# A hybrid decoder layer on one core: two buffers for K and Q, a freed second output tile, an early load for the last tile, S1 x T1 ahead, and statistics that are spread by transposes

## The chip, the cores and the metric

The kernel runs on one core of one Trainium2 chip. The core has a matrix engine (TensorE, PE in the profile, with its weight loads as PEld), a vector engine (VectorE, DVE), a scalar engine (ScalarE, ACT), GpSimd (POOL) and SyncE (SP), which here issues nearly all DMA transfers. Each engine takes its own instructions in order and waits for the others by semaphores. The metric is the time of one execution in microseconds (us) of device time, as the median of several runs. Beside the runs there is one profiled execution, which has its own time.

## The reference

One decoder layer, 2048 tokens by 1024 channels, float32. What is computed, cut to what matters here:

```
u    = rmsnorm(x) ;  proj = u @ w_in          # hq, hf, hi, hg (4 heads x 128 each), att q/k/v
f    = lb + (1 - lb) * sigmoid(hf)            # per head h: q, k = 1 - f, v, log f
S_t  = diag(f_t) S_{t-1} + k_t v_t^T ;  o_t = S_t^T q_t        # HGRN2, four heads
o_hg = rmsnorm(o) * silu(hg)
o_att = sliding-window (128) attention, 8 query heads over 2 key heads, a sink logit per head
h    = x + concat(o_hg, o_att) @ w_out
v    = rmsnorm(h)
gate = causal depthwise conv(v @ w_gate)
h    = h + (silu(gate) * (v @ w_up)) @ w_down
out  = rmsnorm(h)
```

## The kernel before

Activations lie transposed, channels on the 128 partitions and tokens along the free dimension. The sequence is done in two halves of 1024 tokens (`HALF`), one after the other, with the same program; the recurrent state, a key/value block and the convolution's halo are carried over. Every float32 operand of a large product is split into a high and a low part in a reduced format (`split`, `split_into`, `prep`: a cast on ACT, a subtraction on DVE), and a product is then three TensorE instructions (high x high, high x low, low x high), each of 128 x 128 weights by 512 columns.

A half has these stages. (1) The input is loaded and split, and its sum of squares collected. (2) Two key/value units, then for each of four heads a HGRN2 head (`hgrn`) and a pair of attention heads (`attend`), as Python generators that are stepped by turns. (3) `out_proj`: eight output tiles d = 0 to 7, each one `unit` of 48 TensorE instructions (tile `pop`) over the eight mixed tiles M in the order 0, 4, 1, 5, 2, 6, 7, 3; M[3] and M[7] come from the last head (h = 3) and the last attention pair (j = 3). (4) `gate_up`: eleven pairs of feed-forward tiles, each pair a gate and an up product; a pair product (`pair_unit`) computes a 2 x 2 block product in seven products of 12 instructions (a Strassen-Winograd form, with operands B11, T1, B21, T2, T3, B22, T4 on the activation side and A11, S1, A12, S2, S3, S4, A22 on the weight side). (5) `down`: the same form for w_down, with the activations reloaded from device memory, and the final norm.

A HGRN2 head makes K = 1 - f and Q = q * f in two tiles, and then walks seven levels (m = 1, 2, 4 ... 64): at each, ACT copies part of K into G (levels below 32), TensorE multiplies G or K by Q (tile `plev`), and DVE multiplies K and Q by decays and copies the masked result into ST. Afterwards K is transposed (`pkn`), the states are chained (`pu`, SS), and `po` takes ST and Q. K and Q had one buffer each, so a head's Q could only be written after the `po` of the head before. In the attention pair, scores (`psc`) are exponentiated, transposed (`ppt`), masked by DVE into `po` and `pp` (line 395) and multiplied by V (`poT`).

In `out_proj` the input tile of output tile d (`h0` to `h7`, from `xT`) takes one of eight slots of a ring, tag `m`. Weight operands of the gate's first pair are made in the middle of tile d = 6 by `prep_pair`, and one of them, S4's two parts, took a slot of that ring before `h7`; `h7` came after it.

What sets the order: the program is written in one order per engine by a scheduler that simulates a timeline, from the dependencies, the buffers and the order of the code. `tc.issue_after` holds a block behind a given instruction. `AFTER` (line 37) did that for two units of `out_proj`: d = 1 behind level 8 of the last head, d = 2 behind its `po`.

The norm's statistics (`Stats`): squares are added into `acc` over the channels' tiles; `inverse` (lines 232 to 244) sums over partitions on TensorE (`pst`, one column per 128 tokens), takes the inverse root on DVE in thirteen small instructions (`rsqrt`), and writes a diagonal matrix per 128 tokens; `spread` (lines 246 to 255) multiplies ones by it (`pinv`), which puts the tokens' factors on all partitions. For the gate, `inverse` was put ahead of product S2 x T2 of the first pair and `spread` ahead of S4 x B22 (the table `then`, line 762).

Of the kernel before, what the change touches and what calls it, by code (L numbers as in the profile page):

```python
# [17 lines left out]
P = 128  # L18
# [15 lines left out]
QUADS = ["A11", "A12", "A21", "A22"]  # L34
PRODUCTS = [("P1", "A11", "B11"), ("P5", "S1", "T1"), ("P6", "S2", "T2"), ("P3", "S4", "B22"),
            ("P7", "S3", "T3"), ("P2", "A12", "B21"), ("P4", "A22", "T4")]
AFTER = {1: 8, 2: "po"}
LEVELS = [1, 2, 4, 8, 16, 32, 64]
NEG = -1.0e30
UT = 7  # L40
# [5 lines left out]
def hymba_layer(ctx: ExitStack, tc: tile.TileContext, a: dict, out: bass.AP):  # L46
# [18 lines left out]
    def ps(kind, name):  # L65
        return spaces[kind].tile([P, 512], F32, tag=kind, name=name)
# [79 lines left out]
        nc.vector.tensor_scalar(C.omlb, C.lb, -1.0, 1.0, op0=ALU.mult, op1=ALU.add)  # L146


    def rsqrt(ss, n, scale, keep=None):

        ms = sp.tile([P, n], F32, tag=f"ms{n}", name="ms")
        nc.vector.tensor_scalar(ms, ss, scale, EPS, op0=ALU.mult, op1=ALU.add)
        y = sp.tile([P, n], F32, tag=f"y{n}{keep}", name="y")
        yi = y.bitcast(I32)
        nc.vector.tensor_scalar(yi, ms.bitcast(I32), 1, None, op0=ALU.logical_shift_right)
        nc.vector.tensor_scalar(yi, yi, -1.0, float(0x5F3759DF), op0=ALU.mult, op1=ALU.add)
        nc.vector.tensor_scalar(ms, ms, -0.5, None, op0=ALU.mult)
        t = sp.tile([P, n], F32, tag=f"t{n}", name="t")
        for _ in range(3):
            nc.vector.tensor_tensor(t, y, y, op=ALU.mult)  # L160
            nc.vector.tensor_tensor(t, t, ms, op=ALU.mult)
            nc.vector.scalar_tensor_tensor(y, t, 1.5, y, op0=ALU.add, op1=ALU.mult)
        return y

    def raw4(src):
# [49 lines left out]
    class Stats:  # L215
# [16 lines left out]
        def inverse(self, keep):  # L232

            n = self.acc.shape[-1]
            nt = n // P
            st = ps("hg", "pst")
            for c in range(nt):
                nc.tensor.matmul(st[:, c:c + 1], self.acc[:, c * P:(c + 1) * P], ones[:, 0:1],
                                 start=True, stop=True)
            rs = self.rs = rsqrt(st[:, 0:nt], nt, 1.0 / D, keep)  # L240
            dg = self.acc
            return nc.vector.tensor_tensor(dg.rearrange("p (c t) -> p c t", t=P),
                                    ident.unsqueeze(1).to_broadcast([P, nt, P]),
                                    rs.unsqueeze(2).to_broadcast([P, nt, P]), op=ALU.mult)

        def spread(self, bank=None):

            n = self.acc.shape[-1]
            w = min(n, 512)
            for b in range(n // w):  # L250
                pb = ps(aux[b % 2 if bank is None else bank], "pinv")[:, 0:w]
                nc.tensor.matmul(pb, ones, self.acc[:, b * w:(b + 1) * w], start=True, stop=True)
                if bank is not None:
                    return pb
                nc.scalar.copy(self.acc[:, b * w:(b + 1) * w], pb)
# [161 lines left out]
    def hgrn(hf, h, X, invb, vs, WG, mix, p, fu=None):  # L417
# [9 lines left out]
            nc.vector.scalar_tensor_tensor(q[:, bs], qu[b], 128.0 ** -0.5, invb[:, bs], op0=ALU.mult, op1=ALU.mult)  # L427
        nc.vector.tensor_scalar(f, f, C.omlb[:, h:h + 1], C.lb[:, h:h + 1], op0=ALU.mult, op1=ALU.add)
        yield
        K = p.tile([P, HALF], F32, tag="K", name="K", bufs=1)  # L430
        nc.vector.tensor_scalar(K, f, -1.0, 1.0, op0=ALU.mult, op1=ALU.add)
        Q = p.tile([P, HALF], F32, tag="Q", name="Q", bufs=1)
        nc.vector.tensor_tensor(Q, q, f, op=ALU.mult)


# [7 lines left out]
                                    ident.unsqueeze(1).to_broadcast([P, 4, P]), op=ALU.mult)  # L443


        late = h == HG - 2

        def gate():
            gu = unit(WG.get(h, a["w_g"][h]), X, "g")
# [73 lines left out]
                                               op0=ALU.mult, op1=ALU.add)  # L523
        yield
        g = q
        if h < HG - 2:
            gate()
            yield
        on = p.tile([P, TT, P], F32, tag="t4", name="on", bufs=2)
# [74 lines left out]
    def out_proj(hf, M, p):  # L604

        order = [0, 4, 1, 5, 2, 6, 7, 3]
        lo, hi = slice(0, 512), slice(512, HALF)
        acc = inv_tile()
        st = Stats(acc)
        sts = [Stats(acc[:, bs], lambda: p.tile([P, 512], F32, tag="ut", name="sq", bufs=UT)) for _, bs in halves()]  # L610
        ops = Operands(p)
        ops.get("B11", 0)
        kept, v = [], []
        W = [prep(a["w_out"][d], d == 2) for d in range(3)]
        first = None
        for d in range(KT):
            t = slot(f"h{d}")
            nc.sync.dma_start(t, a["xT"][d, :, hf * HALF:(hf + 1) * HALF])
            if d == KT - 2:
                W += [prep(a["w_out"][k]) for k in (d, d + 1)]  # L620

                first = prep_pair(a["w_gate"][0], a["w_gate"][1],
                                  lambda n: p.tile([P, D], F32R, tag="ga", name=n, bufs=2),
                                  lambda n: p.tile([P, 512], F32, tag="ut", name=n, bufs=UT))
            if d >= len(W):
                W.append(prep(a["w_out"][d]))
            with tc.issue_after(marks[AFTER[d]].ins) if d in AFTER else ExitStack():
                o = unit(W[d], M, "pop", order, "at" if d == 2 else "mm", in_turn=d == KT - 1)
            k = dp.tile([P, HALF], F32, name=f"keep{hf}{d}")
            kept.append(k)  # L630
            u = v[d - 4] if d >= 4 else None
            w = [t[:, bs] if d < KT - 1 else p.tile([P, 512], F32, tag="ut", name="v7", bufs=UT) for _, bs in halves()]
            for b, bs in halves():
                nc.vector.tensor_tensor(t[:, bs], t[:, bs], o[b], op=ALU.add)
                sts[b].add(t[:, bs])
                nc.sync.dma_start(k[:, bs], t[:, bs])
                nc.scalar.activation(w[b], t[:, bs], AF.Identity, scale=C.nfw[:, d:d + 1])
                if d >= 4 and b == 0:
                    split_into(*ops.get("B21", d - 4), w[0])
            v.append(t)  # L640
            if d < 4:
                split_into(*ops.get("B11", d), t[:, lo])
                t1 = p.tile([P, 512], F32, tag="ut", name="t1", bufs=UT)
                nc.vector.tensor_tensor(t1, t[:, hi], t[:, lo], op=ALU.subtract)
                split_into(*ops.get("T1", d), t1)
                continue

            nc.vector.tensor_tensor(u[:, hi], w[1], u[:, hi], op=ALU.subtract)
            nc.vector.tensor_tensor(u[:, lo], u[:, hi], u[:, lo], op=ALU.add)
            nc.vector.tensor_tensor(w[0], w[0], u[:, lo], op=ALU.subtract)  # L650
        for op, base, part in (("T2", 0, lo), ("T3", 0, hi), ("B22", 4, hi), ("T4", 4, lo)):
            for i in range(4):
                split_into(*ops.get(op, i), w[op == "B22"] if base + i == KT - 1 else v[base + i][:, part])
        return kept, ops, st, first

    def prep_pair(src1, src2, home=None, ut=None):
# [8 lines left out]
        def m(name, shape=[P, D], dt=F32R):  # L665
            return hp.tile(shape, dt, tag="m", name=name, bufs=KT)
# [22 lines left out]
            split_into(*A, r1)  # L689
        R = ring()  # L690
        split_into(*R, r2)
        dd = m("S4", [P, 2, 512])
        split_into(dd[:, 0], dd[:, 1], S4)
        cut = lambda t, c: (t[0][:, c], t[1][:, c])
        return {"A11": cut(A, lo), "A12": cut(A, hi), "S1": cut(B, lo), "S2": cut(B, hi),
                "S3": cut(R, lo), "A22": cut(R, hi), "S4": (dd[:, 0], dd[:, 1])}

    def pair_unit(W, ops, p, evac, then={}):

        def prod(o, w, t, more=False):
            wh, wl = W[w]
            then.pop(w, lambda: None)()
            for i in range(4):
                xh, xl = ops.get(t, i)
                ws = slice(i * P, (i + 1) * P)
                nc.tensor.matmul(o, wh[:, ws], xh, start=i == 0 and not more, stop=False, skip_group_check=more)  # L708
                nc.tensor.matmul(o, wh[:, ws], xl, start=False, stop=False, skip_group_check=more)  # L709
                nc.tensor.matmul(o, wl[:, ws], xh, start=False, stop=i == 3, skip_group_check=more)  # L710

        def out(o, name):
            t = p.tile([P, 512], F32, tag="ut", name=name, bufs=UT)
            nc.scalar.copy(t, o)  # L714
            return t

        X = ps("mm", "X")
        prod(X, "A11", "B11")
        s1 = out(X, "s1")
        Z = ps("at", "Z")  # L720
        prod(Z, "A12", "B21")
        evac(0, 0, Z, s1)
        prod(X, "S2", "T2", True)
        u2 = out(X, "u2")
        Y = ps("hg", "Y")
        prod(Y, "S1", "T1")
        s5 = out(Y, "s5")
        prod(X, "S3", "T3", True)
        u3 = out(X, "u3")
        evac(1, 1, u3, s5)  # L730
        prod(Y, "S4", "B22", True)
        evac(0, 1, Y, u2)
        prod(X, "A22", "T4", True)
        evac(1, 0, X, None)

    def gate_up(hf, ops, hs, nxt, p):
# [5 lines left out]
        for pr in range(FT // 2):  # L742
# [14 lines left out]
            def flush():  # L757
                while later:
                    later.pop(0)()

            later = []
            then = {"S2": lambda: hs.inverse("h"), "S4": lambda: (hs.spread(), flush())} if pr == 0 else {}
            nxt = prep_pair(srcs[2 * pr + 1][0], srcs[2 * pr + 1][1])
            pair_unit(W, ops, p, gate, then)
            flush()
            ys = []
            for i in range(2):
# [323 lines left out]
```

## Time and profile before

| what | value |
|---|---|
| runs | 2214.91, 2217.16, 2218.22 us; median 2217.16 us |
| profiled execution, its own time | 2213.91 us |
| its span in the trace | 2212.2 us |
| TensorE busy | 2175.0 us (98%) |
| VectorE busy | 1638.0 us (74%) |
| ScalarE busy | 1049.3 us (47%) |
| chain that ended last | PE 95%, DVE 3%, ACT 1%, DMA 1% |
| HBM traffic over the span | 252 MB, 114 GB/s |

How to read it: an engine's busy time counts its instructions, and for TensorE their ends are modelled. Rows of the timeline give the start, the length, the engine and line, the operation with its output and inputs (buffer numbers left out), and in brackets the idle time before it with what ended that. Rows by windows give, for each stretch, the busy time and instruction count of PE, PEld, DVE, ACT and POOL, then the granted TensorE clock (PEclk, 1.00 is full), the DMA share and GB/s. By their columns, the gate of the first half begins at 462 us, that of the second at 1555 us; `out_proj` begins at 343 and 1427 us.

### The profile page before, as it was taken

The numbers are of one execution on the slowest core, as the hardware profiler recorded it, in microseconds if no ns is written. First come the engines' busy times: TensorE is split into PE (matmuls) and PEld (weight loads), VectorE is DVE, ScalarE is ACT, GpSimd is POOL, SyncE is SP. The second block draws the span as 40 slices with busy tenths as digits, with TensorE's granted clock in tenths as the row PEclk, the third lists the DMA queues.
The fourth block names the chain that finished last, engine by engine and source line by source line (L and its number), as shares of the span: only waits on it lengthen the run. The fifth ranks groups of instructions, "written<-read, shape, count | busy, mean of one in ns | idle before, by whom it ended". The sixth has DMA issues, their size and how long they took to land.

```text
span 2212.2 us, 29221 instructions
## 1 busy us (share of the span) xinstructions
PE 2175.0 (98%) x11302; PEld 1822.3 (82%) x11302; DVE 1638.0 (74%) x2458; ACT 1049.3 (47%) x1825; POOL 14.4 (1%) x37
## 2 busy tenths in 40 slices
PE   8999998999999999999999999999999999999997
PEld 6988987778888888888889889878788888888887
DVE  6567567688887888775865666667878888887766
ACT  5445454454444445335725455535534444443353
POOL 2000000000000000000000000000000000000000
PEclk9999999999999999999999999999999999999999
DMA  4111112323333234964631111113232323359643
GB/s 154 39 29 39 29 29 77 108 83 93 113 100 115 87 128 145 376 230 159 203 124 38 30 29 39 59 37 136 64 125 86 125 85 119 95 194 393 220 130 128
DMA packets 89995, 254.15 MB, mean 115 GB/s; under 512 B 11008, under 2 KB 13184, under 8 KB 89856
## 3 DMA queue, kind: packets, MB, share of 16 engines
q1 hardware_dynamic: 87552, 251.17, 34.1%
q8 instruction: 88, 1.44, 0.3%
q10 hardware_dynamic: 2304, 1.12, 0.2%
q14 instruction: 51, 0.42, 0.1%
HBM read 195.10 MB, written 57.15 MB: 114 GB/s over the span
## 4 chain that ended last, share of the span: by engine, by line
PE 95%; DVE 3%; ACT 1%; DMA 1%; issue 0%; ACTq 0%; DVEq 0%
PE X L708 7%; PE X L709 7%; PE X L710 7%; PE pop L197 6%; PE q L197 4%; PE hq L197 4%; PE f L197 4%; PE pdx L890 4%; PE pdx L891 4%; PE Y L708 4%; PE pdx L892 4%; PE Y L710 4%; PE Y L709 4%; PE g L197 4%; PE pdy L891 3%; PE pdy L890 3%
## 5 line engine op out<-in xcount | busy, mean ns | idle before, releaser
L585 ACT CAST whi<-raw 128x1024 fp32r<-128x1024 f32 x88 | 92.7, 1053 | 109.7 <-PE X L709 68.8
L709 PE MATMUL X<-T,whi 128*128 128x512 f32 x352 | 137.4, 390 | 0.0
L708 PE MATMUL X<-T,whi 128*128 128x512 f32 x352 | 137.1, 389 | 0.0
L710 PE MATMUL X<-T,wlo 128*128 128x512 f32 x352 | 137.0, 389 | 0.0
L774 DVE SCALAR_TENSOR_TENSOR y<-ga,cw,y 128x1024 f32<-128x1024 f32 x88 | 112.4, 1277 | 28.2 <-ACT y L772 28.1
L714 ACT COPY u<-X 128x512 f32<-128x512 f32 x88 | 51.5, 585 | 122.3 <-PE X L710 122.2
L586 DVE TENSOR_TENSOR wlo<-raw,whi 128x1024 fp32r<-128x1024 f32 x88 | 107.0, 1216 | 0.0
L586 DVE TENSOR_TENSOR xld<-raw,xhd 128x1024 fp32r<-128x1024 f32 x72 | 80.5, 1129 | 18.9 <-ACT xhd L585 18.3
L178 ACT CAST whi<-raw 128x1024 fp32r<-128x1024 f32 (+2 forms) x61 | 62.9, 1035 | 65.9 <-PE hq L197 11.8
L585 ACT CAST xhd<-raw 128x1024 fp32r<-128x1024 f32 x72 | 69.7, 979 | 40.2 <-DMA raw<-act1T 14.4
L197 PE MATMUL pop<-XH,wlo 128*128 128x512 f32 x256 | 83.3, 391 | 0.7 <-DVE wlo L179 0.7
L197 PE MATMUL pop<-XL,whi 128*128 128x512 f32 x256 | 84.0, 392 | 0.0
L197 PE MATMUL pop<-XH,whi 128*128 128x512 f32 x256 | 82.9, 396 | 0.4 <-ACT XH L208 0.2
L179 DVE TENSOR_TENSOR wlo<-raw,whi 128x1024 fp32r<-128x1024 f32 (+2 forms) x61 | 72.9, 1199 | 13.9 <-ACT whi L178 13.9
L708 PEld LDWEIGHTS X<-T,whi 128*128 128x128 f32 x352 | 66.1, 188 | 14.0 <-ACT u L714 0.3
L710 PEld LDWEIGHTS X<-T,wlo 128*128 128x128 f32 x352 | 66.1, 188 | 13.9 <-issue 0.2
L709 PEld LDWEIGHTS X<-T,whi 128*128 128x128 f32 x352 | 66.1, 188 | 13.8 <-issue 0.2
L890 PE MATMUL pdx<-xhd,hid 128*128 128x512 f32 x192 | 74.4, 391 | 1.0 <-ACT hid L585 1.0
L891 PE MATMUL pdx<-xld,hid 128*128 128x512 f32 x192 | 74.8, 390 | 0.0
L708 PE MATMUL X<-T,Sh 128*128 128x512 f32 x176 | 69.0, 392 | 5.2 <-ACT s L714 5.2
L892 PE MATMUL pdx<-xhd,lod 128*128 128x512 f32 x192 | 73.7, 389 | 0.0
L578 PE MATMUL pvv<-whi,XL 128*128 128x256 f32 x256 | 73.2, 287 | 0.0
(363 smaller groups left out, 6544.5 us busy)
## 6 DMA issues: line engine op xcount, KB each, us to landing
wr<-in_w_down SPq DMA_DIRECT2D x90, 512.0 KB, 5.2
raw<-in_w_gate SPq DMA_DIRECT2D x44, 512.0 KB, 3.7
raw<-in_w_up SPq DMA_DIRECT2D x44, 512.0 KB, 3.6
raw<-act0T SPq DMA_DIRECT2D x20, 512.0 KB, 5.6
raw<-act1T SPq DMA_DIRECT2D x20, 512.0 KB, 5.3
act0B<-y SPq DMA_DIRECT2D x33, 256.0 KB, 2.4
act1B<-y SPq DMA_DIRECT2D x33, 256.0 KB, 2.4
raw<-in_w_out SPq DMA_DIRECT2D x16, 512.0 KB, 3.7
```

The costliest lines, as they stand in the source:

```text
L179: nc.vector.tensor_tensor(lo[:, c], raw[:, c], hi[:, c].bitcast(F32), op=ALU.subtract)
L197: nc.tensor.matmul(o[b], w, x[:, bs], start=f, stop=l)
L578: nc.tensor.matmul(o[:, 0:256], xl[:, t], hi[:, c], start=False, stop=False)
L585: nc.scalar.copy(h, src)
L586: (eng or nc.vector).tensor_tensor(l, src, h.bitcast(F32), op=ALU.subtract)
L708: nc.tensor.matmul(o, wh[:, ws], xh, start=i == 0 and not more, stop=False, skip_group_check=more)
L709: nc.tensor.matmul(o, wh[:, ws], xl, start=False, stop=False, skip_group_check=more)
L710: nc.tensor.matmul(o, wl[:, ws], xh, start=False, stop=i == 3, skip_group_check=more)
L774: nc.vector.scalar_tensor_tensor(y, g[:, w:w + HALF], C.cw[:, ft, w:w + 1], y, op0=ALU.mult, op1=ALU.add)
L890: nc.tensor.matmul(o, wh[:, i, c], ah[:, i, cols], start=f, stop=False, skip_group_check=more)
L891: nc.tensor.matmul(o, wh[:, i, c], al[:, i, cols], start=False, stop=False, skip_group_check=more)
L892: nc.tensor.matmul(o, wl[:, i, c], ah[:, i, cols], start=False, stop=l, skip_group_check=more)
```

## The change

Six edits:

- K and Q have two buffers each.
- `AFTER` no longer holds tile d = 1; tile d = 2 stays behind `po`.
- S4's parts for the gate's first pair get a tile of their own (`dd`), so `h7` takes the ring's slot and its load comes ahead of the last two w_out loads.
- In the first gate pair of each half, S1 x T1 is done directly after A11 x B11, ahead of A12 x B21.
- There `inverse` stands ahead of S3 x T3 and `spread` ahead of A22 x T4, one or two products later than before.
- `inverse` writes no diagonal matrix, and `spread` transposes each column of the inverse roots, read with a step of zero 128 times, in place of the product with ones. This is so for all nine spreads of the program.

Another line (`late`) reads differently and has the same value.

```diff
-AFTER = {1: 8, 2: "po"}
+AFTER = {2: 'po'}
...
         def inverse(self, keep):
...
-            rs = self.rs = rsqrt(st[:, 0:nt], nt, 1.0 / D, keep)
-            dg = self.acc
-            return nc.vector.tensor_tensor(dg.rearrange("p (c t) -> p c t", t=P),
-                                    ident.unsqueeze(1).to_broadcast([P, nt, P]),
-                                    rs.unsqueeze(2).to_broadcast([P, nt, P]), op=ALU.mult)
+            self.rs = rsqrt(st[:, 0:nt], nt, 1.0 / D, keep)
+            return made[-1]
...
-                nc.tensor.matmul(pb, ones, self.acc[:, b * w:(b + 1) * w], start=True, stop=True)
+                for c in range(w // P):
+                    i = b * w // P + c
+                    nc.tensor.transpose(pb[:, c * P:(c + 1) * P], self.rs[:, i:i + 1].to_broadcast([P, P]), ident)
...
-        K = p.tile([P, HALF], F32, tag="K", name="K", bufs=1)
+        K = p.tile([P, HALF], F32, tag="K", name="K", bufs=2)
...
-        Q = p.tile([P, HALF], F32, tag="Q", name="Q", bufs=1)
+        Q = p.tile([P, HALF], F32, tag="Q", name="Q", bufs=2)
...
-        late = h == HG - 2
+        late = h in (2,)
...
-        if h < HG - 2:
+        if not late and h < HG - 1:
             gate()
...
-                                  lambda n: p.tile([P, D], F32R, tag="ga", name=n, bufs=2),
+                                  lambda n, shape=[P, D]: p.tile(shape, F32R, tag="dd" if n == "dd" else "ga", name=n,
+                                                                 bufs=1 if n == "dd" else 2),
...
-        dd = m("S4", [P, 2, 512])
+        dd = (home or m)("dd" if home else "S4", [P, 2, 512])
...
         s1 = out(X, "s1")
+        Y = ps("hg", "Y")
+        if ahead:
+            prod(Y, "S1", "T1")
         Z = ps("at", "Z")
         prod(Z, "A12", "B21")
         evac(0, 0, Z, s1)
         prod(X, "S2", "T2", True)
         u2 = out(X, "u2")
-        Y = ps("hg", "Y")
-        prod(Y, "S1", "T1")
+        if not ahead:
+            prod(Y, "S1", "T1")
...
-            then = {"S2": lambda: hs.inverse("h"), "S4": lambda: (hs.spread(), flush())} if pr == 0 else {}
+            then = {"S3": lambda: hs.inverse("h"), "A22": lambda: (hs.spread(), flush())} if pr == 0 else {}
...
-            pair_unit(W, ops, p, gate, then)
+            pair_unit(W, ops, p, gate, then, pr == 0)
```

The change moves instructions on every engine, since the scheduler orders the whole program anew. Three places matter below.

First, TensorE where the last head's levels and the last attention pair meet the first output tiles, first half. `pop` is an output tile, `plev` a level, `ppt` the transposes of the scores, `poT` their product with V. Before, from the second level on:

```order
L469 MATMUL plev_2943<-Q_2916,G_2944 128x2x64 x4
L392 MATMUL ppt_3337<-ident_87,sc_3028 128x128 x4
L392 MATMUL ppt_3346<-ident_87,sc_3028 128x128 x4
L469 MATMUL plev_2955<-Q_2916,G_2956 128x2x64 x4
L197 MATMUL pop0_3501<-XH_3295,whi_3482 128x512
L197 MATMUL pop1_3502<-XH_3295,whi_3482 128x512
L403 MATMUL poT_3353<-po_3335,V_436 64x128
```

In the change 20 `pop` rows stand between the second `ppt` and the third level, and from there on:

```order
L470 MATMUL plev_2960<-Q_2921,G_2961 128x2x64 x4
L199 MATMUL pop0_3506<-XL_3301,whi_3487 128x512
L199 MATMUL pop1_3507<-XL_3301,whi_3487 128x512
L199 MATMUL pop0_3506<-XH_3300,wlo_3488 128x512
L199 MATMUL pop1_3507<-XH_3300,wlo_3488 128x512
L199 MATMUL pop0_3506<-XH_3304,whi_3487 128x512
L199 MATMUL pop1_3507<-XH_3304,whi_3487 128x512
L199 MATMUL pop0_3575<-XL_3301,whi_3493 128x512
L199 MATMUL pop1_3576<-XL_3301,whi_3493 128x512
L199 MATMUL pop0_3575<-XH_3300,wlo_3494 128x512
L404 MATMUL poT_3358<-po_3340,V_441 64x128
```

So between `ppt` and the first `poT` there were one level and two `pop` instructions, and there are now one level and 29. In the second half it is one level and none before, and one level and 33 now. The number of `pop` instructions ahead of the last head's `po` is 84 in both.

Second, ACT at the start of the gate, first half, where `s1` is the copy of the first product, `sq` and `v7` the square and the weighted form of `h7`'s halves. Before:

```order
L585 CAST Sh_4230<-S_4229 128x1024
L227 ACTIVATE sq_4113<-h7_4057 128x512
L637 ACTIVATE v7_4110<-h7_4057,nfw_325 128x512
L227 ACTIVATE sq_4121<-h7_4057 128x512
L637 ACTIVATE v7_4111<-h7_4057,nfw_325 128x512
L714 COPY s1_4258<-X_4245 128x512
L585 CAST B21_4044<-v7_4110 128x512
```

In the change:

```order
L586 CAST T4_4176<-h6_3950 128x512
L229 ACTIVATE sq_4126<-h7_4062 128x512
L639 ACTIVATE v7_4116<-h7_4062,nfw_325 128x512
L716 COPY s1_4263<-X_4250 128x512
L586 CAST Sh_4235<-S_4234 128x1024
```

The first half of `h7` has moved 14 rows up, between casts of T2, and B21's last cast stands before the copy; 1024 columns of `Sh` have moved behind it.

Third, TensorE at the spread of the gate, first half. Before:

```order
L709 MATMUL X_4245<-T4_4172,whi_3980 128x512
L710 MATMUL X_4245<-T4_4171,wlo_3981 128x512
L708 MATMUL X_4245<-T4_4171,whi_3980 128x512
L252 MATMUL pinv_4344<-invb_3478,ones_83 128x512
L252 MATMUL pinv_4347<-invb_3478,ones_83 128x512
L709 MATMUL X_4245<-T4_4172,whi_3980 128x512
```

In the change:

```order
L710 MATMUL Y_4265<-B22_4164,dd_3989 128x512
L711 MATMUL Y_4265<-B22_4165,dd_3989 128x512
L712 MATMUL Y_4265<-B22_4164,dd_3989 128x512
L253 MATMUL pinv_4361<-ident_87,y_4319 128x128 x4
L253 MATMUL pinv_4367<-ident_87,y_4319 128x128 x4
L710 MATMUL Z_4445<-B21_3861,whi_4230 128x512
L711 MATMUL Z_4445<-B21_3862,whi_4230 128x512
```

Two products of 512 columns have become eight transposes of 128. Before, they stood near the end of A22 x T4; now they stand directly behind S4 x B22.

More of the change, by code (lines that the diff above doesn't have):

```diff
@@ L146, in constants @@
         nc.vector.tensor_scalar(C.omlb, C.lb, -1.0, 1.0, op0=ALU.mult, op1=ALU.add)
+    made = []
     def rsqrt(ss, n, scale, keep=None):
@@ L161, in rsqrt @@
             nc.vector.tensor_tensor(t, t, ms, op=ALU.mult)
-            nc.vector.scalar_tensor_tensor(y, t, 1.5, y, op0=ALU.add, op1=ALU.mult)
+            made.append(nc.vector.scalar_tensor_tensor(y, t, 1.5, y, op0=ALU.add, op1=ALU.mult))
         return y
@@ L696, in prep_pair, with pair_unit @@
                 "S3": cut(R, lo), "A22": cut(R, hi), "S4": (dd[:, 0], dd[:, 1])}
-    def pair_unit(W, ops, p, evac, then={}):
+    def pair_unit(W, ops, p, evac, then={}, ahead=False):
         def prod(o, w, t, more=False):
```

## The prediction

> **What bounds the kernel now.** I read the page first (span, busy times, the chain by engine).
>
> ```profile
> span 2212.2 us, 29221 instructions
> PE 2175.0 (98%) x11302; PEld 1822.3 (82%) x11302; DVE 1638.0 (74%) x2458; ACT 1049.3 (47%) x1825; POOL 14.4 (1%) x37
> PE 95%; DVE 3%; ACT 1%; DMA 1%; issue 0%; ACTq 0%; DVEq 0%
> ```
>
> TensorE is the bound: 37.2 us of the span are not PE. A gain can come from three places only: idle time of PE, stretches at a low granted clock, and PE instructions that go. So I went through the span by windows (columns as told above), looking for stretches that are not full:
>
> ```profile
> 351.00:355.00 4.00, 2.73 (x22) 2.23 (x20) 4.00 (x8) 3.74 (x6) 0.00 (x0) 1.00 0.00 0
> 355.00:358.80 3.80, 0.66 (x4) 0.19 (x2) 3.80 (x6) 0.11 (x1) 0.00 (x0) 1.00 0.00 0
> 358.80:362.20 3.40, 3.30 (x28) 2.87 (x27) 3.40 (x6) 0.62 (x1) 0.00 (x0) 0.50 0.00 0
> 377.00:381.00 4.00, 3.04 (x67) 2.52 (x61) 3.96 (x8) 1.30 (x3) 0.00 (x0) 1.00 0.00 0
> 462.24:484.60 22.36, 19.54 (x92) 15.59 (x91) 21.32 (x42) 12.97 (x23) 0.00 (x0) 1.00 0.26 90
> 550.00:600.00 50.00, 50.00 (x222) 41.41 (x221) 42.73 (x57) 21.17 (x30) 0.00 (x0) 1.00 0.37 122
> 1446.00:1451.00 5.00, 2.51 (x17) 1.71 (x16) 5.00 (x8) 2.19 (x3) 0.00 (x0) 1.00 0.00 0
> 1451.00:1454.40 3.40, 3.40 (x28) 2.81 (x30) 3.40 (x5) 0.56 (x1) 0.00 (x0) 0.50 0.16 16
> 1560.00:1562.60 2.60, 0.01 (x1) 0.01 (x1) 2.60 (x5) 2.60 (x6) 0.00 (x0) 1.00 0.53 202
> 1563.70:1567.10 3.40, 3.40 (x13) 2.82 (x11) 3.40 (x7) 0.62 (x1) 0.00 (x0) 0.50 0.31 122
> 1600.00:1650.00 50.00, 50.00 (x222) 41.44 (x221) 42.04 (x56) 20.17 (x29) 0.00 (x0) 1.00 0.38 123
> ```
>
> The gate away from its start is full, 222 products in 50 us or 0.225 us each (0.227 between starts in the rows below). The holes lie where the last head meets the first output tiles (351 and 1446) and where the gate begins (462 and 1560). After three of these four waits the granted clock is 0.50 for 3.4 us, which costs a further 1.7 us each. Those are the two places at which the change moves instructions.
>
> **T1: last head and first output tiles.** The timeline of the first half, and then of the second:
>
> ```profile
> 322.02 1.23 DVE L433 TENSOR_TENSOR Q<-hg,f 128x1024 f32<-128x1024 f32 x1 [3.50 <-PE po L537]
> 351.63 1.09 PE L392 MATMUL ppt<-ident,sc 128*128 128x128 f32 x8 [0.25 <-DVE sc L365]
> 356.47 0.68 DVE L395 TENSOR_TENSOR po<-ppt,ownT 128x512 f32<-128x512 f32 x1
> 358.50 1.41 PE L403 MATMUL poT<-po,V 128*64 128x128 f32 x7 [3.14 <-DVE pp L395]
> 1445.58 1.03 PE L392 MATMUL ppt<-ident,sc 128*128 128x128 f32 x8
> 1450.97 0.98 PE L403 MATMUL poT<-po,V 128*64 128x128 f32 x3 [2.33 <-DVE pp L395]
> ```
>
> From the last transpose (351.63 + 1.09 = 352.72) to the masked scores' first use (358.50) DVE needs 5.8 us, full all the while, and PE has one level and two output products. In the second half it is 1446.61 to 1450.97, 4.4 us, with no product. The freed tile d = 1 puts 29 and 33 products there: 29 x 0.227 = 6.6 us with a level of some 1 us behind or among them is 7.6, and 33 x 0.227 + 1 is 8.5. Both are longer than DVE's time, so the waits of 3.14 and 2.33 us should go, with the clock that follows them. Idle in 351.00 to 362.20 is 1.27 + 3.14 + 0.10 = 4.5 us; in 1446.00 to 1451.00 it is 2.5.
>
> The number of output products ahead of the head's end stays 84, so what is pulled forward is missing later, between levels 32 and 64 and the second `poT`, where 377.00 to 381.00 already shows 0.96 us idle. I charge two late DVE instructions of about 0.6 us there in the first half (1.2) and one and a half in the second (0.9): my estimate. First half 4.5 + 1.7 - 1.2 = 5.0; second 2.5 + 1.7 - 0.9 = 3.3. **T1 = 8.3.** Low end: the idle time only moves in small pieces and just the two half-clock stretches go, 3.4. High end: nothing new, and the 0.96 goes too: 4.5 + 2.5 + 3.4 + 1.0 = 11.4. A loss I exclude for this term, since no PE instruction is added.
>
> The second buffer for Q lets DVE write it in the 3.50 us in which it waited for the last head's `po`: 1.23 us of DVE earlier. PE had products then, so on its own I price it at nothing; it is part of why DVE is ahead in T1. K goes with it.
>
> **T2: start of the gate.**
>
> ```profile
> 458.34 3.70 DVE L586 TENSOR_TENSOR T<-h,T 128x512 fp32r<-128x512 f32 x6 [0.16 <-ACT T L585]
> 460.86 0.33 SPq L618 DMA_DIRECT2D h<-in_xT  x1
> 462.24 0.39 PE L708 MATMUL X<-B,whi 128*128 128x512 f32 x1
> 469.16 0.56 ACT L714 COPY s<-X 128x512 f32<-128x512 f32 x1
> 469.78 0.50 PE L708 MATMUL X<-T,Sh 128*128 128x512 f32 x1 [2.61 <-ACT s L714]
> 472.20 0.95 PE L238 MATMUL pst<-ones,invb 128*128 128x1 f32 x8
> 484.22 0.39 PE L710 MATMUL Y<-B,S 128*128 128x512 f32 x1
> ```
>
> PE had 9 of A12 x B21's products and then waited 2.61 us for S2 x T2, because `s1`'s copy stood on ACT behind the squares and the weighted form of both halves of `h7`. In the change 12 products of S1 x T1 and all 12 of A12 x B21 come between: 24 x 0.227 = 5.4 us instead of 2.0, and the copy stands behind only one half of `h7`.
>
> From 462.24 to the end of S4 x B22 (484.45) lie 22.2 us: 74 products x 0.227 = 16.8, the two `pst` groups at about 0.95 (1.9), 2.6 of wait and 0.9 of smaller losses. In the change 84 products stand up to that point, ten of which came later before. So at most 2.6 + 0.9 = 3.5 us per half can go. But DVE is busy 21.32 of 22.36 us here, so the next things to be late are its products: the next pair's `wlo` (DVE has some 21 instructions of 0.62 and three of about 1.2 from 458.34, so about 475, where PE wants it at 474) and the last part of T2 (about 478). I charge 0.9 for them: 3.5 - 0.9 = 2.6 in the first half; in the second the same and 1.7 of half clock, 4.3. **T2 = 6.9.** Low end: 2.0 us more of each wait come back, which is 0.6 + 0.6 + 1.7 = 2.9; high end 3.5 + 3.5 + 1.7 = 8.7. Statistics placed one or two products later have the same instructions; what waits for them is ACT's evacuations, of which the next is behind A22 x T4, so I price them at nothing as long as PE has the next pair.
>
> The load of `h7` is one issue on SP (460.86 before), now ahead of the last two w_out loads. It delays these by 0.33 us, and they wait for free slots, which DVE and ACT give, not for the queue: nothing.
>
> **T3: spreads.** The groups of three lines, and one spread as it runs:
>
> ```profile
> 43.38 1.88 PE L252 MATMUL pinv<-invb,ones 128*128 128x512 f32 x4
> L252 PE MATMUL pinv<-invb,ones x22: 379/592/797, 43.4 to 2203.4; 128*128 128x512 f32 x18, 128*128 128x256 f32 x4
> L252 PE MATMUL pinv<-sums,ones x4: 590/590/592, 1108.9 to 1125.2; 128*128 128x512 f32 x4
> L392 PE MATMUL ppt<-ident,sc x128: 270/273/329, 126.0 to 1465.5; 128*128 128x128 f32 x128
> L392 PEld LDWEIGHTS ppt<-ident,sc x128: 137/140/144, 125.8 to 1465.4; 128*128 128x128 f32 x128
> L242 DVE TENSOR_TENSOR invb<-ident,y x7: 425/1222/1226, 37.1 to 2202.3; 128x1024 f32<-128x1024 f32 x4, 128x256 f32<-128x256 f32 x2, 128x512 f32<-128x512 f32 x1
> ```
>
> A float32 product of 512 columns is two instructions in the trace (four for 1024 tokens), and they start (1.88 - 0.59) / 3 = 0.43 us apart. 18 + 4 of them are 9.4 us of PE. They are eleven products of 512 tokens, so 44 transposes. One transpose lasts 0.273 us, but eight take 1.03 us: 0.129 each with the last one's whole length, 0.108 from start to start. 44 x 0.129 = 5.7. **T3 = 9.4 - 5.7 = 3.7.** High end 9.4 - 44 x 0.108 = 4.6. Low end: not overlapped, 44 x 0.273 = 12.0, a loss of 2.6. A weight read with a step of zero is not in the trace; a load of 0.140 is, and even 0.140 + 0.273 in series loses only 44 x 0.413 - 9.4 = 8.8. I take the row of the same form, the overlapped one. The nine diagonals leave DVE, but all except the tail's lie beside PE work and count nothing.
>
> [...]
>
> **T4: tail.** The last spread, of 256 tokens:
>
> ```profile
> 2200.00:2212.20 12.20, 1.70 (x4) 0.58 (x3) 7.67 (x30) 0.00 (x0) 0.00 (x0) 0.58 0.50 172
> 2202.33 0.42 DVE L242 TENSOR_TENSOR invb<-ident,y 128x256 f32<-128x256 f32 x1
> 2202.81 1.22 PE L252 MATMUL pinv<-invb,ones 128*128 128x256 f32 x2 [2.33 <-DVE invb L242]
> ```
>
> PE waits here for the diagonal; its 0.42 us go; two transposes at the low clock (0.58) take the place of a product, which I charge 0.07: **T4 = 0.35**, between 0 and 0.5.
>
> **Sum.** 8.3 + 6.9 + 3.7 + 0.35 = 19.25 us off the profiled run's own 2213.91: 2194.7. The runs' median is 3.25 above it: 2197.9, say 2198. The ends sum to 3.7 and 25.2, so 2213.5 and 2192.
>
> **Rivals.**
> A, *the waits move only*. DVE is full in both places (4.00 of 4.00, 21.32 of 22.36), and what it makes is not less, apart from Q and the diagonals; then PE waits for it a little later, in pieces, and T1 and T2 stand at their low ends: 3.4 + 2.9 + 3.7 + 0.35 = 10.35, so 2206.8. Against it: most of what DVE makes there is for later use, and PE has its 84 products to spend. Chance 0.14.
> B, *transposes do not overlap* (T3 = -2.6): 8.3 + 6.9 - 2.6 + 0.35 = 12.95, 2204.2. For it: the operand with a step of zero is new; against it, the rows of L392. Chance 0.07. [...]
> C, *slower*: the whole program is ordered anew, and about twelve pair units of the second half get another order of products on TensorE, of 84 x 0.227 = 19.1 us each. If in each of them an operand came late by more than 19.25 / 12 = 1.6 us, the gain would be gone; at 2 us each it is 24, so 2222. For it: waits of 2.6 us by such an order exist (469.78). Against it: both halves have different orders before, and both are 50.00 of 50.00. Chance 0.04.
> D, *more goes*: no new wait, the high ends, 25.2, so 2192. Chance 0.06.
> That the change doesn't do what it says is out for T1 to T3, since the rows of the order show it.
>
> **How the numbers follow.** The forecast has 0.69 and, with T1 and T2 off by half of their distance to the ends, its own range 2193 to 2203. The range 2191 to 2209 takes in A, B and D and leaves C and a low end of everything. A measurement of this kernel tells about 0.2% (4.4 us) from none: slower than that holds C, 0.04; no change holds the part of A and B in which both come together and the sum is under 4.4, 0.04; faster holds the rest, 0.92.
>
> **What would show it.** T1: windows from 351 and from 1446 with PE full and clock 1.00, and new waits before the second `poT` of at most 0.7 us each. T2: no row of S2 x T2 with over 1 us of idle time after ACT's `s1`, clock 1.00 through the second half's start, and idle time below 1 us in the 22 us after the gate's first product. T3: eight transposes in about 1 us at each spread (2 us and more is B), no rows of diagonals on DVE. T4: the last spread's wait about 0.4 us shorter. I am wrong if 351 or 1446 keep a half-clock stretch, if the gate's wait stands again at another operand at its full 2.6 us (A), or if 1600 to 1650 is no longer 50.00 of 50.00 (C).

## The result, and the profile after

The changed kernel runs in 2195.71 us (median of 4 runs, 2195.61 to 2195.83) against 2217.18 us before (4 runs, 2214.91 to 2218.22). The ratio is 0.9905, with a 95% interval of 0.9887 to 0.9922: 21.5 us or just under 1% faster. The prediction was 2198, in a range of 2191 to 2209. The profiled execution of the changed kernel took 2195.79 us, its span 2194.1, which is 18.1 us less than the span before.

The page of the changed kernel, span, busy times and chain by engine:

```profile
span 2194.1 us, 29255 instructions
PE 2165.0 (99%) x11324; PEld 1815.4 (83%) x11324; DVE 1629.2 (74%) x2449; ACT 1048.5 (48%) x1825; POOL 13.3 (1%) x37
PE 94%; DVE 3%; DMA 1%; ACT 1%; issue 1%; SPq 0%; DVEq 0%; ACTq 0%
```

37.2 us of the span were not PE; 29.1 are now. PE's own busy time fell by 10 us, which I estimate to be mostly the spreads (4.6 by their spacing) and the half-clock stretches (up to 1.7 each) together.

The windows of the changed kernel that answer to those of before (start and end, then busy PE, PEld, DVE, ACT, POOL, granted clock, DMA share, GB/s):

```profile
350.00:354.60 4.60, 4.60 (x29) 4.01 (x28) 4.60 (x6) 2.06 (x3) 0.00 (x0) 1.00 0.00 0
354.60:362.20 7.60, 7.60 (x39) 5.94 (x37) 6.28 (x13) 3.16 (x9) 0.00 (x0) 1.00 0.46 140
454.71:477.51 22.80, 21.80 (x101) 17.43 (x100) 19.81 (x41) 13.44 (x24) 0.00 (x0) 1.00 0.19 59
550.00:600.00 50.00, 50.00 (x223) 41.39 (x222) 39.55 (x51) 23.57 (x34) 0.00 (x0) 1.00 0.29 90
1436.00:1446.00 10.00, 10.00 (x54) 8.51 (x53) 10.00 (x16) 3.53 (x5) 0.00 (x0) 1.00 0.33 94
1541.00:1564.00 23.00, 22.02 (x103) 17.58 (x102) 19.95 (x41) 13.57 (x24) 0.00 (x0) 1.00 0.19 57
1600.00:1650.00 50.00, 50.00 (x222) 41.43 (x221) 39.77 (x51) 23.67 (x35) 0.00 (x0) 1.00 0.28 91
```

The stretch behind the scores' transposes (350 to 362, and 1436 to 1446) is full in both halves. The gate's start has 1.0 us of idle time in each half. None of these stretches is at half clock; behind the start, the clock is below 1.00 only in the tail (0.52 from 2182.00 to the end). First the transposes of the scores and the first product with V, then some of the waits that are left and the gate's spread, by the timeline of the changed kernel:

```profile
351.06 1.03 PE L393 MATMUL ppt<-ident,sc 128*128 128x128 f32 x8
359.54 0.43 PE L404 MATMUL poT<-po,V 128*64 128x128 f32 x2
369.22 1.09 PE L393 MATMUL ppt<-ident,sc 128*128 128x128 f32 x8 [0.49 <-DVE sc L384]
379.81 0.49 PE L537 MATMUL po<-v,ST 128*128 128x128 f32 x2 [0.52 <-ACT on L539]
470.45 0.50 PE L711 MATMUL X<-T,Sh 128*128 128x512 f32 x1 [0.30 <-DVE T L587]
471.86 0.50 PE L710 MATMUL X<-T,whi 128*128 128x512 f32 x1 [0.68 <-ACT u L716]
477.51 1.03 PE L253 MATMUL pinv<-ident,y 128*128 128x128 f32 x8
2184.67 0.69 PE L253 MATMUL pinv<-ident,y 128*128 128x128 f32 x2 [2.15 <-DVE y L164]
```

Between the start (6.69 us for the first input, before and after) and the tail (1.42 and 2.15 us) no wait is longer than 0.7 us. Between landmarks that both traces have (first and last instruction of a stage on PE), the 18.1 us come from these places:

| from ... to | first half | second half |
|---|---|---|
| heads and out_proj, from behind the input norm to the last output product (T1) | 6.0 | 3.2 |
| of this, from the first output product on | 5.6 | 2.5 |
| gate_up, the spread's 0.84 taken off (T2) | 1.7 | 2.7 |
| spreads (T3), all together, with 0.9 lost around the second half's start | 3.4 | |
| tail (T4) | 0.4 | |
| first products of the program, not of the change | 0.7 | |

The last row is not the change's doing. Before, seven of the program's first products start 0.43 us apart in place of 0.23; now three do. These products, the first key/value units, end at 32.9 us before and at 32.2 now, and between 31.6 and 34.9 over all 14 profiles, though no edit touches them.

### The profile page after: what moved, and what is told of

Its sections match the earlier page's. It is cut to its first block, busy times and chain, and to the rows that moved or that the text cites. A ratio compares the mean times of both kernels' runs of the same rounds, so it can differ in the third digit from the quotient of the medians.

```text
span 2194.1 us, 29255 instructions
## 1 busy us (share of the span) xinstructions
PE 2165.0 (99%) x11324; PEld 1815.4 (83%) x11324; DVE 1629.2 (74%) x2449; ACT 1048.5 (48%) x1825; POOL 13.3 (1%) x37
## 4 chain that ended last, share of the span: by engine, by line
PE 94%; DVE 3%; DMA 1%; ACT 1%; issue 1%; SPq 0%; DVEq 0%; ACTq 0%
PE X L711 7%; PE X L710 7%; PE X L712 7%; PE pop L199 7%; PE hq L199 4%; PE g L199 4%; PE q L199 4%; PE f L199 4%; PE Y L710 4%; PE Y L712 4%; PE Y L711 4%; PE pdx L895 3%; PE pdx L896 3%; PE pdx L897 3%; PE pdy L896 3%; PE pdy L895 3%
## 5 line engine op out<-in xcount | busy, mean ns | idle before, releaser
L578 PE MATMUL pvv<-whi,XH 128*128 128x256 f32 x256 | 72.4, 284 | 0.0
```

## The experiments

Each kernel is the one before with some of the six edits, or the whole change with one thing different. Each stands beside runs of the kernel before, whose median was 2216.1 to 2216.7. The ratio is not that of the two medians, so the last two columns can differ a little.

| label | what it has | median, us | less than before, us | ratio and 95% interval |
|---|---|---|---|---|
| e1_spread | spreads by transposes | 2212.26 | 3.9 | 0.9984 (0.9975 to 0.9993) |
| e2_tile1 | d = 1 not held | 2209.87 | 6.3 | 0.9968 (0.9955 to 0.9980) |
| e3_kq | two buffers for K and Q | 2215.52 | 0.7 | 1.0002 (0.9993 to 1.0011) |
| e10_q_tile1 | d = 1 not held, two buffers for Q | 2208.09 | 8.7 | 0.9958 (0.9946 to 0.9971) |
| e5_kq_tile1 | d = 1 not held, two for K and Q | 2204.24 | 11.9 | 0.9949 (0.9937 to 0.9962) |
| e4_gate | the three edits at the gate | 2210.81 | 5.4 | 0.9973 (0.9963 to 0.9983) |
| e6_h7 | h7's early load alone | 2211.11 | 5.0 | 0.9976 (0.9967 to 0.9985) |
| e7_ahead | S1 x T1 ahead alone | 2213.14 | 3.0 | 0.9987 (0.9978 to 0.9996) |
| e8_later | statistics later alone | 2214.09 | 2.0 | 0.9990 (0.9982 to 0.9999) |
| e11_tile2 | whole change, d = 2 not held either | 2209.93 | 6.8 | 0.9968 (0.9955 to 0.9980) |
| e12_h7_only | whole change, only h7's edit at the gate | 2195.61 | 21.1 | 0.9903 (0.9888 to 0.9918) |

The three places add up: 3.9 (spreads) + 11.9 (last head) + 5.4 (gate) = 21.2, where the whole change gives 21.5. By the intervals each of the three is known to about 2 to 3 us.

### The spreads

```diff
...
-                nc.tensor.matmul(pb, ones, self.acc[:, b * w:(b + 1) * w], start=True, stop=True)
+                for c in range(w // P):
+                    i = b * w // P + c
+                    nc.tensor.transpose(pb[:, c * P:(c + 1) * P], self.rs[:, i:i + 1].to_broadcast([P, P]), ident)
```

> Before, with the nine spreads done by transposes and the diagonal matrices gone, nothing else. My theory (transposes overlap, 0.108 to 0.129 us each): 3.7 + 0.35 = 4 us less than before, between 3 and 5; in the trace eight transposes start within 0.9 us, the last spread's wait shorter by the diagonal's 0.42 us. Rival B (they stand one behind the other, or load slowly): 2 us slower or more. Rival 'spreads lie beside a wait anyway': 1 us less or no change.

Measured: 3.9 us less. The group of the spreads in the changed kernel, by its line (minimum, median and maximum of one in ns):

```profile
L253 PEld LDWEIGHTS pinv<-ident,y x48: 132/137/227, 41.1 to 2184.7; 128*128 128x128 f32 x48
L253 PE MATMUL pinv<-ident,y x48: 270/272/474, 41.3 to 2184.9; 128*128 128x128 f32 x48
```

An operand read with a step of zero cost no more here than another: its weight load takes 137 ns, where the scores' took 140, and eight transposes take 1.03 us from first start to last end, as at the scores. Rival B falls. From start to start it is 0.11 us, so 1024 tokens take 0.87 us of PE in place of the 1.71 of four products. In the trace of e1_spread the last spread's wait is only 0.18 us shorter (2.15 for 2.33), not 0.42.

### The last head: tile d = 1 and the buffers

```diff
-AFTER = {1: 8, 2: "po"}
+AFTER = {2: "po"}
```

> Before, with output tile d = 1 no longer held behind level 8; K and Q with one buffer each. In the order 32 output products now stand between the last transposes of the scores and their first use, in both halves. My theory (the products fill the wait, the buffers matter little): 8 us less, from T1, no half-clock stretch at 358 or at 1451. Rival 'the buffers make it': the wait moves to where Q is late, 3.4 us or less gained. Rival 'DVE is the limit, waits only move': 3.4 us.

> Before, with two buffers for K and Q, nothing else; the order has 15 output products between the last transposes and their first use in the first half and 9 in the second, where before had 2 and none (my count of rows). My theory: the buffers by themselves are worth nothing, but the order that comes with them fills a part of the wait: 15 x 0.227 = 3.4 us of DVE's 5.8 in the first half, so 3 us less or so in all, the half-clock stretch perhaps gone. Rival 'nothing': within 1 us of before. Rival 'the buffers are the change': 8 us less.

> Before, with both edits at the last head: two buffers for K and Q and tile d = 1 not held. Tile d = 1 alone gained 6.3 us, the buffers alone nothing. Theory 'the buffers free DVE, which then is less late for the products in place': more than the sum, 9 to 12 us less, since edits at the gate (5.4) and at the spreads (3.9) leave 12 of the whole change's 21.4. Rival 'each edit counts by itself': 6 to 7 us less, and the rest of the 21.4 comes from the three places acting together.

> Before, with tile d = 1 not held and a second buffer for Q alone; K keeps one. With neither buffer it was 6.3 us less than before, with both 11.9. Theory 'Q's write behind the last head's po is what makes DVE late': 10 to 12 us less. Rival 'K is needed too': 6 to 8 us less.

Measured: tile d = 1 alone 6.3 us less, the buffers alone none (the interval holds 1), both 11.9, and with Q's second buffer but not K's 8.7. So e2_tile1 fell short of its 8, e3_kq of its 3, and e10_q_tile1 lies between its two expectations, so K's buffer counts too. Alone, the buffers do not fill the wait. The trace of e3_kq has two output products between the last transposes and their first use in each half, as before has, and not the 15 and 9 of the expectation. In the first half the wait is split, as the waits of PE in e3_kq from 350 to 363 show (total, times, longest):

```profile
PE poT L403 <- DVE pp L395: 1.3, 1, 1.3
PE pop L197 <- ACT XH L208: 0.8, 1, 0.8
PE plev L469 <- DVE Q L476: 0.7, 1, 0.7
PE poT L403 <- DVE po L395: 0.7, 1, 0.7
```

These sum to 3.5 us where before had 3.14 at one place and 1.0 at a level, so this order bought little; in the second half the wait was 3.1 us, longer than the 2.33 before, and 6.8 us of half clock followed. With d = 1 not held, the large wait is gone, and what is left for the buffers is seen in the waits of e2_tile1 (343 to 392), PE's and one of DVE's (300 to 392):

```profile
PE po L536 <- ACT on L538: 1.0, 2, 0.5
PE po L536 <- DVE SS L522: 0.7, 1, 0.7
PE ppt L392 <- DVE sc L383: 0.5, 1, 0.5
PE poT L403 <- DVE pp L395: 0.4, 2, 0.3
PE plev L469 <- DVE Q L476: 0.3, 1, 0.3
...
DVE Q L433 <- PE po L537: 3.5, 1, 3.5
```

and in those of e5_kq_tile1 (340 to 386):

```profile
PE po L536 <- ACT on L538: 1.0, 2, 0.5
PE ppt L392 <- DVE sc L383: 0.5, 1, 0.5
PE plev L482 <- DVE K L486: 0.2, 1, 0.2
PE poT L403 <- DVE pp L395: 0.2, 1, 0.2
```

DVE's wait of 3.5 us for the `po` of the head before, which stood in e2_tile1 as it did before, is gone with Q's second buffer, and so is PE's wait for a level's Q (0.3). In e10_q_tile1, which has that buffer alone, PE still waits 0.7 us for the states (SS) and 0.4 for `pp`; with K's buffer as well the first goes and the second is halved. By the landmarks of the profiles, the heads and out_proj of the first half gain 4.1 us with d = 1 alone, 4.8 with Q's buffer and 5.9 with both; the second half 3.0, 3.6 and 3.3. So the buffers are worth about 2 us here by the traces and 5.6 by the medians. About half of the 2 us (0.4 and 0.7) lies ahead of the first output product, and e3_kq gains as much there. In the two profiles a further 3.2 us lie at the second half's gate, where both kernels still have the old wait: in e2_tile1 it was followed by 6.8 us of half clock, in e5_kq_tile1 by none (last section). That the medians differ for this reason is argued, not shown.

### The gate

```diff
-        dd = m("S4", [P, 2, 512])
+        dd = (home or m)("dd" if home else "S4", [P, 2, 512])
...
+        if ahead:
+            prod(Y, "S1", "T1")
...
-            then = {"S2": lambda: hs.inverse("h"), "S4": lambda: (hs.spread(), flush())} if pr == 0 else {}
+            then = {"S3": lambda: hs.inverse("h"), "A22": lambda: (hs.spread(), flush())} if pr == 0 else {}
```

> Before, with the three edits at the gate alone: S4's parts in a tile of their own with h7's load early, S1 x T1 ahead in the first pair, statistics one or two products later. My theory: the wait of 2.61 us at S2 x T2 goes in both halves and 0.9 to 1.5 us of it come back at other operands, with 1.7 us of half clock in the second half: 5 to 7 us less. Rival A (waits only move): 2.9 us less.

> Before, with S4's parts in a tile of their own and h7's load early, nothing else at the gate. The order alone now has 12 products of S1 x T1 and all of A12 x B21 ahead of S2 x T2, as in the whole change. Theory 'what counts is how many products lie between A11 x B11 and S2 x T2': as the three edits together, 4 to 6 us less. Rival 'each edit is worth a part': 1 to 3 us less.

> Before, with S1 x T1 written directly after A11 x B11 in the first pair, nothing else at the gate; h7 stays late. 12 + 9 products lie ahead of S2 x T2, 21 x 0.227 = 4.8 us, which is just the time from A11 x B11's end (464.96) to the wait's end (469.78). Theory 'number of products': 4 to 6 us less, wait under 0.5 us. Rival 'the late h7 is the cause': a wait of 1 us or more stays, at S2 x T2 or S1 x T1, and 0 to 2 us are gained.

> Before, with the statistics one or two products later, nothing else. The order has 9 products of A12 x B21 and 12 of S1 x T1 ahead of S2 x T2, 4.8 us again. Theory 'number of products': 4 to 6 us less. Rival 'statistics off the path are worth nothing': no change.

> The whole change without two of its gate edits: S1 x T1 stands in its old place in the code and the statistics where they were; h7's early load stays. By itself h7's load gained 5.0 of the 5.4 us of the three. Theory 'the early x is what counts, the other two only move the order': within 0.5 us of the whole change. Rival 'each is worth its own 2 to 3 us': 2 us or more slower than the whole change.

Measured: the three together 5.4, h7's edit alone 5.0, S1 x T1 ahead alone 3.0, the later statistics alone 2.0; and the whole change without the last two is as fast as with them (2195.61 and 2195.71). With h7's edit in place the other two add nothing; the whole change without h7's edit was not run. e7_ahead and e8_later, with 3.0 and 2.0, fit neither of their two expectations. Each of the three makes the scheduler put S1 x T1's products ahead of S2 x T2, and in each the row of 2.61 us is gone. But where h7 stays late, waits come a little further on. The waits of PE in e7_ahead, and the cast on ACT that the first of them waits for, by its timeline:

```profile
473.28 1.04 ACT L585 CAST whi<-raw 128x1024 fp32r<-128x1024 f32 x1 [1.05 <-PE Z L709]
474.38 0.50 PE L708 MATMUL X<-B,whi 128*128 128x512 f32 x1 [0.90 <-ACT whi L585]
475.85 0.50 PE L710 MATMUL X<-B,wlo 128*128 128x512 f32 x1 [0.45 <-DVE wlo L586]
479.59 0.50 PE L708 MATMUL X<-T,whi 128*128 128x512 f32 x1 [0.67 <-ACT u L714]
```

This is 2.0 us in three pieces. The first two are the next pair's weights: ACT's cast waited 1.05 us for A12 x B21's last products, which here stand behind nine of S2 x T2's (their B21 is made from h7), and DVE's `wlo` follows the cast. The third stands in the whole change as well (471.86). By the landmarks of the first half e7_ahead gains 0.4 us at the gate, e8_later 0.5, e6_h7 and e4_gate 1.6. Rival A of the prediction, the waits only move, is what these two edits do. What they gain by the medians is more; a likely reason is that the short waits were followed by no half clock in their two profiles, and one of 2.6 us was in some.

### Beyond the change: tile d = 2

```diff
-AFTER = {2: 'po'}
+AFTER = {}
```

> The whole change, and tile d = 2 not held behind po either. In the order some 40 products of d = 2 now stand between the last attention's product with V and the states' chain. Theory 'products fill waits wherever they stand': the wait of 0.86 us behind the states in the second half goes, but as many products are then missing later; 0 to 1 us less than the whole change. Rival 'they hold the chain up': DVE and ACT get the states 9 us later and the stage ends later, 2 us or more slower than the whole change.

Measured: 2209.93, 14 us slower than the whole change. The theory misses and the rival holds, at seven times its least of 2 us. Some 40 products of d = 2 stand ahead of the chain of states, and they are missing at the stage's end. The windows of e11_tile2, then one row of its timeline:

```profile
375.00:394.60 19.60, 18.72 (x112) 15.77 (x108) 4.01 (x12) 4.61 (x19) 0.00 (x0) 1.00 0.00 0
394.60:399.00 4.40, 1.49 (x8) 1.13 (x8) 3.77 (x15) 0.04 (x1) 0.00 (x0) 0.89 0.00 0
399.00:405.80 6.80, 6.36 (x17) 4.88 (x17) 4.35 (x7) 2.30 (x4) 0.00 (x0) 0.57 0.48 157
```

```profile
397.51 1.68 PE L551 MATMUL pot<-ident,on 128*128 128x128 f32 x8 [3.69 <-DVE on L546]
```

From 375 PE is nearly full and DVE is busy for 4.0 of 19.6 us only, since what DVE needs comes from the chain that the products hold up. Then PE waits 3.7 us for DVE's norm of the head's output, with nothing to fill it, and runs 6.8 us at half clock behind that. The first half loses 6.0 us against the whole change, the second 8.3. Products fill a wait only where they do not delay the chain that ends the stage; the hold of d = 2 behind `po` is what keeps them for its end. None of these kernels is faster than the changed one beyond the scatter of its runs.

### The kernel before once more

> The kernel before, unchanged, profiled once more. Its runs lie between 2213.2 and 2219.1, its profiled run at 2213.91 had three half-clock stretches of 3.4 us besides the tail. Theory 'the spread of the runs is half-clock stretches that come or don't after the waits at 355, 467, 1449 and 1560': the profile's time differs from 2213.91 by 1.7 us for each 3.4 us of half clock more or less, after the start's difference (up to 2 us) is taken off. Rival 'the spread is the start's or DMA': the same stretches and another time.

Measured: 2215.6 us, 1.69 more than the first profile, with the same half-clock stretches at the same waits. The theory misses here and the rival holds: by the landmarks 1.0 us was lost in the first products of the program (the first input 0.3 us later, a wait for weights of 0.8 us for 0.4, and two more products 0.43 us apart) and the rest around the second half's start. So 1.7 us between two runs come without any difference in half clock behind the four waits; how much of the other runs' spread is half clock stays open.

## Why the prediction came out as it did

**The bound and the places** were right: outside of the two places, the spreads and the tail there are 0.7 us at the start, 1.1 in the heads ahead of the first output product and a loss of 0.9 around the second half's start, and 550 to 600 and 1600 to 1650 are still 50.00 of 50.00. Rival C (slower by another order) did not happen.

**T1**, forecast 8.3, is 9.2 in the profile, 8.1 of it at the place itself: from the first output product on 5.6 for 5.0 and 2.5 for 3.3. The mechanism was right: 29 and 33 products cover DVE's 5.8 and 4.4 us, and from the last transposes to the first product with V it is now 7.45 and 8.35 us, where 7.6 and 8.5 were worked out. (The second half was not without a product there before, as the order's account and the prediction have it: its trace shows two, at 1446.77.)

The step that failed is "on its own I price it at nothing" for the buffers, if it is read as their part in the change: alone they are nothing in the median, but with the freed tile they are worth 2 us by the traces. Two other terms were too large and cancel in part, which is luck. The late DVE instructions were charged with 1.2 and 0.9 us; idle time between these products with V and the last head's `po` rose by 0.1 in the first half (0.96 to 1.03) and by 1.2 in the second (0.24 to 1.44). The half clock was priced at 1.7 each. From the first output product to the gate's first one, the first half takes 118.4 us in e7_ahead, whose profile has no half clock there, and 119.1 to 120.0 in the five profiles with the same wait and 3.4 us of it; the second half takes 117.1 in e4_gate without and 117.4 to 118.8 in six with it. By these differences it cost 0.2 to 1.6 us, and 1.7 in none.

**T2**, forecast 6.9, is 4.4: 1.7 and 2.7 where 2.6 and 4.3 were forecast. The term for new waits was too small. "I charge 0.9 for them" was to stand against 3.5 us of waits and smaller losses; the new waits are 1.3 us longer than a product's normal spacing (0.46 for T2's last part, 0.84 for ACT's copy of the product before S3 x T3, which I had not listed), and behind each of these two the next product starts 0.34 and 0.33 us later in place of 0.23, so a further wait costs another 0.1 at its restart. The half clock's 1.7 in the second half was 1.0: before, `gate_up` takes 430.84 us there from its first product to its last, and 429.84 to 429.88 in the six halves (before, e2_tile1, e3_kq, e5_kq_tile1) that have the wait without half clock. "In the second the same" was wrong in a detail too: the stretch idles 2.82 us in the first half and 2.62 in the second. Nor is the half clock a property of the place: of 14 such waits in the profiles of kernels that have it, 5 were followed by half clock. And three edits were described as one step; with h7's in place the other two add nothing.

**T3**, forecast 3.7, is 3.4 by landmarks, with the loss of 0.9 around the second half's start in it, and 4.6 by the spacing of 0.11 us (the high end I had not taken); e1_spread measured 3.9 with the tail. The 272 ns of the group's row are the length of one, and not what one adds among others.

**T4**: the tail is 0.4 us shorter for 0.35. Of this 0.18 shows as a shorter last wait; the spread ahead of it also ends 0.27 us sooner.

**The sum** was 19.25 against the profile's 18.1, so 1.1 too much; without the 0.7 us that the start gave by chance, the four terms are 17.4, and the sum was 1.8 too much. The median came out lower than predicted all the same, 2195.71 for 2198, because of the last step: "the runs' median is 3.25 above it". That offset was carried over to the changed kernel, and it belonged to the kernel before, whose runs lie between 2213.2 and 2220.1. The changed kernel's runs lie within 0.22 us, and its profiled run is one of them (2195.79). Errors of opposite sign, 1.1 and 3.3, make the 2.2 us, so that the forecast comes this near is luck in part. Of the rivals, A holds for two of the gate's three edits, B for none, and D did not come about: new waits did come at the gate, whose idle time of 1.00 and 0.98 us is just at the limit that the prediction had set.

## What to carry to other kernels

Move independent work into a wait only after asking which chain ends the stage: some 30 products from a later tile paid 6.3 us, and 11.9 with the buffers, where DVE was behind anyway, and 40 from the next tile cost 14 where they held that chain up. When several edits aim at one wait, try each alone and all but one: here the edit for one early load did the work, and the two others mostly moved the wait. A sum made on one profiled execution should carry the offset to the median only if the cause of that offset survives the change.

## What the runs showed of the hardware

The half clock after a wait came in steps of 3.4 us, and not each time. In the 11 profiles of kernels that still have waits of over 2 us at these places, a wait is followed by no half clock, by 3.4 us or by 6.8 us of it. The windows of e2_tile1 and of e10_q_tile1 at the gate of the second half, behind the same wait of 2.6 us that before had 3.4 us of half clock after it and e5_kq_tile1 had none:

```profile
1557.75:1564.55 6.80, 6.80 (x21) 5.64 (x21) 4.83 (x9) 1.86 (x3) 0.00 (x0) 0.52 0.09 34
```

```profile
1557.75:1564.55 6.80, 6.80 (x23) 5.69 (x21) 5.63 (x10) 1.85 (x3) 0.00 (x0) 0.51 0.08 33
```

At 0.5 of the clock for 6.8 us such a stretch can cost 3.4 us, an estimate: half of its length. By the length of `gate_up` it cost 3.2 (e2_tile1) and 2.6 (e10_q_tile1) against the 429.8 us without half clock, and a stretch of 3.4 us cost 1.0 (before, e9_before) and 1.5 (e10_q_tile1, first half). Behind the gate's wait half clock came in 5 of 14 places (7 profiles, two halves); behind the waits at the last head in 14 of 16. These are single waits of 2.3 to 3.2 us but for the first half of e3_kq, where pieces of at most 1.3 us had it too. The shortest of the four waits, 2.33 us at 1450.97 in the profile of before, has it in 6 of its 7 profiles, the gate's of 2.6 us in 5 of 14: length alone did not decide. What else does, and where the steps of 3.4 us come from, no run here shows.

That half clock followed some of these waits and not others would explain, though it is argued and not shown, why the kernels without waits of over 1 us between start and tail scatter so little: the changed kernel and e12_h7_only lie within 0.2 and 0.7 us over four runs each, all others within 3 to 8 us over 5 to 11. It does not explain the start, which differs by up to 3.3 us between profiles. In these profiles such a wait cost its length and, where half clock followed it, by the differences above 0.2 to 3.2 us more.
